# Weights times values of two attentions in plain float32, two heads side by side

## The chip, the cores and the metric

The kernel runs on one core of a Trainium2 chip. A core has a tensor engine (PE: matmuls, and PEld, its loading of the stationary operand), three engines for elementwise work (DVE, ACT and POOL) and queues of DMA. The engines run beside each other, each takes its own instructions in order, and semaphores join them. TensorE's clock has two levels, 1.2 and 2.4 GHz; the profile gives the granted share, 1.0 being 2.4. The metric is the device time of the whole program in microseconds.

## The reference, cut to what matters

Two transformer blocks over 512 tokens of 1024 features, in float32. The change lies in the two attentions of the second block, in the product of the weights with the values:

```python
# stick-breaking attention, 16 heads of 64
z = q k' / 8
log_1m = where(key < query, log_sigmoid(-z), 0)
a = where(key < query, exp(log_sigmoid(z) + sum of log_1m over later keys), 0)
o = einsum('bhqs,bshd->bqhd', a, v)                  # here

# compressed, selected and windowed attention, 16 heads in 4 groups of keys
o_cmp = einsum('bghqn,bngd->bqghd', p_cmp, v_cmp)    # here
o_sel = einsum('bghqkl,bgqkld->bqghd', p_sel, v_sel) # here
o_win = einsum('bghqs,bsgd->bqghd', p_w, v_w)        # here
out = (gate_0 o_cmp + gate_1 o_sel + gate_2 o_win) @ w_o
```

With 512 keys, the selected and the windowed attention are both causal attention over keys and values of their own (b = 0 and 1 in the kernel).

## The kernel before, in words

Features or keys lie on the 128 partitions, tokens in the free dimension. TensorE has a fast float32 (float32r, `F32R`) that takes numbers of fewer bits; the kernel makes a float32 product of it by splitting each operand into a high part (ACT copies and rounds, `xh`, `wh`) and a low part (the rest by subtraction, `xl`, `wl`) and adding three products. A matmul whose operands are plain `F32` is float32 as it stands; the profile records it as two matmuls. Weights of the projections come in 512 KB pieces (`Weights`, L303 to 369): SP issues the load of `ws`, ACT makes `wh` (L341), and DVE, for a few pieces POOL, `wl` (L350), both two pieces ahead of their use.

**Stick-breaking attention** (`s_all`). `S_ORDER` writes the order of the work out by hand: step i runs through the parts from left to right, and a part with number n handles head i - n. Each engine takes its instructions in that order. A head i of step i: the projection of queries or keys for a later pair of heads (`sproj`, 24 matmuls, evacuated by `st`, L1616, and split into `sq` or `kk`), scores on the lower triangle as 1280 columns in two parts `za` and `zb` (`s_scores`), cap at 30 (`s_cap`, DVE, L1664 and L1665), exp and ln (`s_exp`, ACT, L1670 and L1671), maximum with the scores (`s_soft`, DVE, L1677 and L1678), high parts (`s_high`, POOL, L1686 to L1688), low parts (`s_low`, L1690: 512 columns on POOL and 768 on DVE, by `low2`, L1718). One step later `s_weights` adds sums of these on PE (`sph`, `spl`), and `s_a` takes exp into `sA` (ACT, L1724 and L1725). `s_ahigh` (POOL, L1731) and `s_alow` (POOL 512 and DVE 640 columns, L1718) split the weights into `sah` and `sal`; `s_values` splits the values into `sv`, 64 columns of high parts beside 64 of low. `s_out` makes the products: for three of four blocks of keys one matmul with `sah` and one with `sal`, each 128 columns of `sv`; for the last a float32 one with `sA`. High values' products lie on partitions 0 to 63 and low values' on 64 to 127; `join` copies the one half (ACT, L1764) and adds the other (DVE, L1765). After the last heads comes the output projection, whose first products (`start`, placed by `S_LEAD` and `S_SPLIT`) stand between the steps of heads 14 and 15.

**Compressed, selected and windowed attention** (`n_attend`). A step is a chunk c of 128 queries of a head h for one of two b; chunks go in the order 3, 2, 0, 1 with 512, 384, 128 and 256 keys. `ORDER` has the parts: scores (two float32r matmuls), `n_bias` (DVE, L2094: mask, and the least), `n_exp` (ACT, L2099), `n_sums` (DVE, reciprocal), `n_scale` (POOL, L2108: gate over sum), `n_turn` (PE, L2116: transposes), `n_high` (ACT, L2126) and `n_low` (DVE, L2130), which split the transposed weights into `pts` or `pth` and `ptl`, and after the last chunk `n_out`, with two matmuls for each of four blocks of keys and two for the compressed weights (`cph`, `cpl`). `join` follows for each head, `n_head` for each pair. `g_query` prepares the queries of a pair, an instruction in each step; POOL makes their low parts (L2075). Every fourth head a step for the compressed scores (`c_`...) opens a group.

Of the kernel before, what the change touches and what calls it, by code (L numbers as in the profile page):

```python
# [18 lines left out]
P = 128  # L19
# [206 lines left out]
def _constants():  # L226
    """Tables that depend on the shapes alone: name -> [128, n]."""
# [143 lines left out]
class Norm:  # L371
    """One over the root of the mean square over the features, for tokens in the free dimension.

    The factor is applied to what the products give, so that they need not wait for it."""

    def __init__(self, s, eps, name, n=T, apart=False):
        """apart: the last squares are summed on their own."""
# [17 lines left out]
    def mean(self, src=None, more=None):  # L395
        """Mean squares with tokens on partitions, [128, chunks], before eps."""
# [32 lines left out]
    def bcast(self, tm=None, tag="rbc", bufs=2):  # L429
        """The factor along the free dimension, the same on every partition."""  # L430
# [13 lines left out]
class Norm2:  # L444
    """The norm that ends the first block and the one that opens the second, as one factor."""
# [22 lines left out]
class Kernel:  # L468
# [19 lines left out]
    def open_banks(self, stack, pool):  # L488
        """PSUM: a pool of eight banks, or banks by their places."""
# [66 lines left out]
    def group(self, ps, w, xh, xl, ks, first, last, m=P):  # L556
        """Accumulate into ps over the k tiles ks: three products of the parts."""
# [49 lines left out]
    def proj_tokens(self, name, xh, xl, chunks):  # L607
        """Products with tokens on partitions: a bank of 512 columns for each chunk."""
# [16 lines left out]
    def resid(self, k, ps, norm, gain, x):  # L625
        """Add to the residual, and what the next products need of it."""
# [13 lines left out]
    # ---- the whole  # L640
# [68 lines left out]
    # ---- block 1: state space and pooling mixer  # L709

    def _mix(self):
# [8 lines left out]
        # B0, C0 and dt come first, each as soon as what it needs is there  # L720
# [66 lines left out]
    def g_z(self, j, ps):  # L787
        """y silu(z) = y (z / 2) (1 + tanh(z / 2))"""
# [53 lines left out]
    def setup(self):  # L842
        """Tables of the state space part."""
# [17 lines left out]
    def select(self, k):  # L861
        """The rows of both heads of a pair, for 64 features each."""
# [3 lines left out]
    def stage(self, n=1):  # L866
        """A step of what runs beside the projections, at most n pairs of heads among it."""
# [14 lines left out]
    def conv(self, name=None, ps=None):  # L882
        """The next step of three convolutions under way, the middle one's first."""
# [1369 lines left out]
```

## Time and profile before

| | us |
|---|---|
| median of 3 runs (2264.5 to 2266.25) | 2265.91 |
| the profiled execution's span | 2262.3 |
| PE busy | 2161.9 |
| DVE busy | 1305.9 |
| ACT busy | 910.6 |
| POOL busy | 544.6 |

The profile is of one execution. Busy is the time in which at least one instruction of the engine ran; a matmul's record goes on after the next has begun, so spacings from start to start tell more of PE than durations. Stages are told by the time from the start of the span: stick-breaking attention with projections from 951 to about 1112 us, its end to about 1153, the compressed, selected and windowed attention from 1680 to 1848.5. A row with an arrow in brackets gives the time that the engine stood before it, and what ended that.

### The profile page before, as it was taken

What the parts mean: (1) busy time and instruction counts of PE and PEld (TensorE: products, weight loads), DVE (VectorE), ACT (ScalarE), POOL (GpSimd) and SP (SyncE); (2) the same over time, 40 slices, a digit from 0 to 9 for tenths busy, and PEclk for the clock granted to TensorE, in tenths of its full rate; (3) what the DMA queues carried; (4) which work ended last, traced back from release to release, by engine and by line L of the source; (5) the groups of instructions that cost most, each with busy time, mean ns of one, the idle gap of its engine ahead of it and who ended that gap; (6) DMA issues with size and microseconds to landing.
All of it is one profiled execution on the core that took longest, in us unless ns stands there. A gap on an engine that the chain in (4) does not pass through costs nothing.

```text
span 2262.3 us, 27154 instructions
## 1 busy us (share of the span) xinstructions
PE 2161.9 (96%) x10250; PEld 1776.0 (79%) x10250; DVE 1305.9 (58%) x2058; ACT 910.6 (40%) x1485; POOL 544.6 (24%) x559
## 2 busy tenths in 40 slices
PE   8899999999999999999899999999888899999998
PEld 5677888788888887777778888887677778888886
DVE  6988756454433335589965343445768875534333
ACT  4333534343322224366544332332448864423222
POOL 3333401111110104166630000013448851000001
PEclk9999999999999999999999999999899999999999
DMA  4222434122332223322233323323331113333231
GB/s 136 67 64 73 140 106 152 59 66 94 101 103 93 93 89 98 121 65 66 56 106 100 103 93 94 102 93 121 106 108 30 31 43 117 93 103 95 94 101 65
DMA packets 63379, 206.09 MB, mean 91 GB/s; under 512 B 7440, under 2 KB 8336, under 8 KB 63120
## 3 DMA queue, kind: packets, MB, share of 16 engines
q1 hardware_dynamic: 59504, 196.99, 27.8%
q10 hardware_dynamic: 3744, 7.37, 0.9%
q8 instruction: 80, 1.31, 0.2%
q14 instruction: 51, 0.42, 0.1%
HBM read 189.39 MB, written 6.29 MB: 86 GB/s over the span
## 4 chain that ended last, share of the span: by engine, by line
PE 68%; DVE 15%; ACT 7%; issue 5%; POOL 4%; DMA 1%; ACTq 0%; POOLq 0%; DVEq 0%
PE psum L540 53%; PE b L540 13%; DVE wl L350 2%; DVE spl L1718 1%; ACT wh L341 1%; DVE t L908 1%; POOL np L2108 1%; ACT sT L1670 1%; ACT sT L1671 1%; DVE pv L1089 1%; DVE xl L553 1%; POOL cx L1832 1%; PE psum L2116 1%; ACT xh L552 1%; DVE pts L2130 1%
## 5 line engine op out<-in xcount | busy, mean ns | idle before, releaser
L540 PE MATMUL psum<-xh,wh 128*128 128x512 f32 x1560 | 611.6, 392 | 2.3 <-ACT sA L1725 1.3
L540 PE MATMUL psum<-xh,wl 128*128 128x512 f32 x1560 | 609.4, 391 | 1.8 <-DVE wl L350 1.5
L540 PE MATMUL psum<-xl,wh 128*128 128x512 f32 x1560 | 608.8, 390 | 0.0
L341 ACT ACTIVATE wh<-ws 128x1024 fp32r<-128x1024 f32 (+1 forms) x346 | 356.3, 1038 | 384.8 <-PE psum L540 321.5
L350 DVE TENSOR_TENSOR wl<-ws,wh 128x1024 fp32r<-128x1024 f32 (+2 forms) x332 | 421.1, 1274 | 86.1 <-ACT wh L341 85.4
L540 PEld LDWEIGHTS psum<-xh,wl 128*128 128x128 f32 x1560 | 293.1, 188 | 66.3 <-DVE wl L350 4.3
L540 PEld LDWEIGHTS psum<-xh,wh 128*128 128x128 f32 x1560 | 293.3, 188 | 63.4 <-issue 1.8
L540 PEld LDWEIGHTS psum<-xl,wh 128*128 128x128 f32 x1560 | 293.3, 188 | 60.9 <-DVE xl L550 0.2
L540 PE MATMUL b<-xh,wh 128*128 128x512 f32 (+1 forms) x488 | 196.1, 402 | 8.4 <-ACT wh L341 6.6
L540 PE MATMUL b<-xh,wl 128*128 128x512 f32 (+1 forms) x488 | 193.6, 397 | 3.8 <-POOL wl L350 1.9
L540 PE MATMUL b<-xl,wh 128*128 128x512 f32 (+1 forms) x488 | 193.7, 397 | 0.5 <-DVE xl L553 0.5
L1357 DVE TENSOR_TENSOR h<-h,psum 128x512 f32<-128x512 f32 x48 | 33.1, 689 | 161.2 <-PE psum L540 161.2
L540 PE MATMUL psum<-hh,wh 128*128 128x512 f32 x320 | 125.1, 391 | 0.0
L540 PE MATMUL psum<-hh,wl 128*128 128x512 f32 x320 | 124.7, 390 | 0.0
L540 PE MATMUL psum<-hl,wh 128*128 128x512 f32 x320 | 124.6, 389 | 0.0
L1348 ACT ACTIVATE t<-t 128x512 f32<-128x512 f32 x64 | 40.5, 632 | 188.9 <-DVE t L1347 188.9
L540 PEld LDWEIGHTS b<-xh,wh 128*128 128x128 f32 (+1 forms) x488 | 92.9, 190 | 28.4 <-ACT wh L341 6.6
L540 PEld LDWEIGHTS b<-xh,wl 128*128 128x128 f32 (+1 forms) x488 | 92.8, 190 | 26.6 <-DVE wl L350 3.3
L553 DVE SCALAR_TENSOR_TENSOR xl<-h,cols,xh 128x512 fp32r<-128x512 f32 x64 | 76.6, 1212 | 61.9 <-ACT xh L552 61.9
L540 PEld LDWEIGHTS b<-xl,wh 128*128 128x128 f32 (+1 forms) x488 | 92.9, 190 | 20.5 <-DVE xl L553 1.2
L392 POOL TENSOR_TENSOR acc_final<-acc_final,sq_final 128x512 f32<-128x512 f32 x6 | 10.4, 1733 | 336.1 <-ACT sq_final L388 336.1
L1287 POOL TENSOR_TENSOR t<-t,t 128x512 f32<-128x512 f32 x22 | 28.4, 1290 | 257.2 <-DVE t L1282 232.7
(515 smaller groups left out, 3510.6 us busy)
## 6 DMA issues: line engine op xcount, KB each, us to landing
ws<-in_wst SPq DMA_DIRECT2D x332, 512.0 KB, 3.4
h<-in_xT SPq DMA_DIRECT2D x16, 256.0 KB, 3.7
kk<-kk SPq DMA_DIRECT2D x16, 256.0 KB, 3.4
nq<-nq SPq DMA_DIRECT2D x16, 256.0 KB, 2.9
ws<-in_wst SPq DMA_DIRECT2D x8, 384.0 KB, 3.1
spill<-back SPq DMA_DIRECT2D x8, 256.0 KB, 2.0
back<-spill ACTq DMA_DIRECT2D x8, 256.0 KB, 3.5
spill<-h ACTq DMA_DIRECT2D x8, 256.0 KB, 5.9
```

What stands on the lines that cost most here:

```text
L341: self.nc.scalar.activation(hi[:, :n], s, AF.Copy)
L350: e.tensor_tensor(lo[:, :n], s, hi[:, :n].bitcast(F32), op=ALU.subtract)
L540: self.nc.tensor.matmul(ps, a, b, start=start, stop=stop, skip_group_check=again)
L552: nc.scalar.activation(hi, src, AF.Copy, scale=scale)
L553: nc.vector.scalar_tensor_tensor(lo, src, scale, hi.bitcast(F32), op0=ALU.mult, op1=ALU.subtract)
L908: nc.vector.scalar_tensor_tensor(t, u[:, q:q + T], cw[:, q:q + 1], t, op0=ALU.mult, op1=ALU.add)
L1089: nc.vector.tensor_tensor(o[:, a:], src[:, a:], src[:, a - n:528 - n], op=ALU.add)
L1287: nc.gpsimd.tensor_tensor(t, t, gate[0], op=ALU.mult)
L1348: nc.scalar.activation(t, t, AF.Square)
L1357: nc.vector.tensor_tensor(self.h[:, m, :], self.h[:, m, :], ps, op=ALU.add)
L1670: self.nc.scalar.activation(t, t, AF.Exp)
L1671: self.nc.scalar.activation(t, t, AF.Ln, bias=1.0)
```

## The change

- The products of weights and values take plain float32 operands: `sA` and `vf` in the first attention, `pt`, `cp`, `vs` and `vc` in the second. The splits `s_ahigh`, `s_alow`, `s_values`, `n_low`, `c_low` and those of the values are gone, and so are `join` and `add`.
- Two heads share a bank: each matmul has 64 columns of values, and the second head's output lies on partitions 64 to 127. They are made once for two heads, after the second of them. In the first attention one ACT copy (`s_join`) then takes both heads, in the second `split` makes the high and low parts of both straight from the bank.
- `s_low` runs on POOL alone, all 1280 columns.
- In the second attention the order of the work is: two heads for b = 0, then the same two for b = 1. The transposed weights are moved by DVE for chunks 1 and 2 and by ACT for 0 and 3 (`n_move`). The low parts of the queries go from POOL (two halves) to DVE (one instruction).
- `sA` has four buffers instead of two; `pt` has three sets.

```diff
-    S_ORDER = (("proj", 0), ("scores", 0), ("low", 1), ("evac", 0), ("cap", 0), ("alow", 2),
+    S_ORDER = (("proj", 0), ("scores", 0), ("low", 1), ("evac", 0), ("cap", 0),
                ("qparts", 0), ("kparts", 0), ("exp", 0), ("soft", 0), ("high", 0),
-               ("weights", 1), ("a", 1), ("ahigh", 1), ("out", 2), ("values", 1), ("join", 2),
-               ("add", 2))
-    S_LEAD = ((14, "proj"), (14, "add"), (15, "alow"), (15, "values"), (17, "kparts"))
+               ("weights", 1), ("a", 1), ("out", 2), ("join", 2))
+    S_LEAD = ((14, "proj"), (14, "join"), (15, "cap"), (15, "out"), (17, "kparts"))
...
     def s_low(self, i):
-        self.low2(lo, t, hi, self.S_POOL[0])
+        self.nc.gpsimd.tensor_tensor(lo, t, hi.bitcast(F32), op=ALU.subtract)
...
     def s_out(self, i):
-        a, ah, al = self.hd[i]
-        vv = self.sv.pop(i)
+        if i % 2 == 0:
+            return
         ps = self.bank("bo")
-        for j in range(3):
-            v = vv[:, j, :]
+        for j in range(4):
             w = 512 - P * j
             s = slice(self.OFF[j], self.OFF[j] + w)
-            self.mm(ps[:, P * j:], v, ah[:, s], j == 0, False)
-            self.mm(ps[:, P * j:], v, al[:, s], False, False)
-        self.mm(ps[:, 384:], vv[:, 3, :].bitcast(F32), a[:, 1152:], False, True)
+            for e in range(2):
+                u = i - 1 + e
+                self.mm(ps[64 * e:64 * e + 64, P * j:], self.vf[:, j, u, :], self.hd[u][:, s],
+                        j == 0, j == 3)
...
-    ORDER = (("scores", 0), ("out", 7), ("join", 9), ("bias", 1), ("turn", 4), ("exp", 2), ("add", 9),
-             ("sums", 2), ("low", 6), ("tick", 0), ("high", 5), ("scale", 2), ("head", 13))
+    ORDER = (("scores", 0), ("out", 7), ("head", 9), ("bias", 1), ("turn", 4), ("exp", 2),
+             ("sums", 2), ("tick", 0), ("move", 5), ("scale", 2))
...
-            for s in halves:
-                nc.gpsimd.tensor_tensor(q[r, 1, s], qr[r, s], q[r, 0, s].bitcast(F32),
-                                        op=ALU.subtract)
-                yield
+            nc.vector.tensor_tensor(q[r, 1, :], qr[r, :], q[r, 0, :].bitcast(F32),
+                                    op=ALU.subtract)
...
+        if c in (1, 2):
+            self.nc.vector.tensor_copy(dst, src)
+        else:
+            self.nc.scalar.activation(dst, src, AF.Copy)
...
     def n_out(self, u):
-        if u["c"] != self.QORD[3]:
+        if u["c"] != self.QORD[3] or h % 2 == 0:
             return
...
+            for e in range(2):
+                self.mm(self.av[halves[e]], vc[:, (h - 1 + e) % 4, :], cp, True, False)
+        pt = [self.pt.pop((h - 1 + e, b)) for e in range(2)]
         for j in range(4):
-            for part in pt:
-                self.mm(self.av[:, P * j:], self.vs[:, b, j, g, :],
-                        part[:, 4 * j:3 * j + 4, :].rearrange("p c q -> p (c q)"),
-                        False, b == 1 and j == 3 and part is pt[1])
+            for e in range(2):
+                self.mm(self.av[halves[e], P * j:], self.vs[:, b, j, g, :],
+                        pt[e][:, 4 * j:3 * j + 4, :].rearrange("p c q -> p (c q)"),
+                        False, b == 1 and j == 3)
```

## Rows read from the trace of the kernel before

**Rows 1.** Stretches: us, busy (x count) of PE, PEld, DVE, ACT, POOL; clock, DMA, GB/s.
```profile
951.00:1112.00 161.00, 151.41 (x775) 121.03 (x773) 143.10 (x161) 95.58 (x124) 98.51 (x81) 0.98 0.23 66
...
1680.00:1848.50 168.50, 146.07 (x926) 119.40 (x926) 148.11 (x573) 145.72 (x427) 134.66 (x205) 0.99 0.13 30
1725.20:1767.10 41.90, 36.80 (x236) 29.95 (x237) 37.06 (x145) 36.95 (x109) 34.98 (x55) 1.00 0.13 28
```
**Rows 2.** Timeline, one step of the first attention: start us, us, instruction, [idle before].
```profile
1028.41 0.39 PE L540 MATMUL psum<-sq,kk 128*128 128x512 f32 x1
...
1030.06 0.39 PE L540 MATMUL psum<-sph,none 128*128 128x384 f32 x1
...
1030.88 0.45 PE L540 MATMUL psum<-spl,none 128*128 128x384 f32 x1 [0.44 <-DVE spl L1718]
...
1032.99 1.27 ACT L1670 ACTIVATE sT<-sT 128x1280 f32<-128x1280 f32 x1 [0.24 <-DVE sT L1665]
1033.08 0.48 PE L540 MATMUL psum<-sah,sv 128*128 128x512 f32 x1
...
1038.44 1.27 POOL L1688 TENSOR_SCALAR sph<-sT 128x1280 fp32r<-128x1280 f32 x1
1038.93 1.85 DVE L350 TENSOR_TENSOR wl<-ws,wh 128x1024 fp32r<-128x1024 f32 x1 [0.41 <-ACT wh L341]
1039.68 2.12 POOL L1731 TENSOR_SCALAR sah<-sA 128x1152 fp32r<-128x1152 f32 x1
1040.18 0.39 PE L540 MATMUL psum<-sq,kk 128*128 128x512 f32 x1
```
**Rows 3.** Timeline of PE, two places with 64-column float32 weights.
```profile
99.23 0.39 PE L540 MATMUL b<-xl,wh 128*128 128x512 f32 x1
99.46 0.39 PE L540 MATMUL b<-xh,wl 128*128 128x512 f32 x1
99.78 1.09 PE L540 MATMUL b<-d,xc 128*64 128x128 f32 x16
100.80 0.94 PE L540 MATMUL b<-ct,prev 128*128 128x128 f32 x6
...
1641.54 0.66 PE L540 MATMUL psum<-hidt,cols 128*64 128x128 f32 x8 [1.52 <-DVE hidt L1869]
```
**Rows 4.** Groups by line, whole span: count | busy us, mean ns | idle before.
```profile
L350 POOL TENSOR_TENSOR wl<-ws,wh 128x1024 fp32r<-128x1024 f32 x14 | 35.1, 2505 | 141.3 <-ACT wh L341 141.3
...
L1718 POOL TENSOR_TENSOR sal<-sA,sah 128x512 fp32r<-128x512 f32 x16 | 21.2, 1326 | 0.1
...
L350 DVE TENSOR_TENSOR wl<-ws,wh 128x1024 fp32r<-128x1024 f32 (+2 forms) x332 | 421.1, 1274 | 86.1 <-ACT wh L341 85.4
```
**Rows 5.** Timeline of PE, end of the first attention.
```profile
1100.69 0.39 PE L540 MATMUL psum<-sph,none 128*128 128x384 f32 x1
...
1108.53 0.77 PE L540 MATMUL psum<-sq,kk 128*128 128x512 f32 x1 [3.04 <-ACT h L1764]
...
1145.51 0.38 PE L540 MATMUL psum<-sA,sv 128*128 128x128 f32 x2
```
**Rows 6.** Stretches, columns as in rows 1: two behind a stop.
```profile
1107.60:1117.70 10.10, 8.81 (x30) 7.12 (x31) 9.80 (x12) 6.41 (x10) 6.95 (x6) 0.50 0.10 31
...
1643.50:1646.80 3.30, 3.30 (x12) 2.82 (x12) 2.87 (x4) 2.26 (x3) 0.00 (x0) 0.50 0.06 11
```
**Rows 7.** Groups by line, one group of four heads, 1725.2 to 1767.1.
```profile
L2130 DVE TENSOR_TENSOR ptl<-psum,pth 128x512 fp32r<-128x512 f32 (+3 forms) x16 | 7.6, 472 | 0.0
...
L1765 DVE TENSOR_TENSOR h<-h,psum 64x512 f32<-64x512 f32 x4 | 2.7, 678 | 0.1
...
L2126 ACT ACTIVATE pts<-psum 128x512 fp32r<-128x512 f32 (+3 forms) x16 | 6.8, 427 | 0.3
...
L1764 ACT ACTIVATE h<-psum 64x512 f32<-64x512 f32 x4 | 2.4, 594 | 0.1
...
L2075 POOL TENSOR_TENSOR nq<-qr,nq 64x256 fp32r<-64x256 f32 x8 | 5.8, 728 | 0.3
```

More of the change, by code (lines that the diff above doesn't have):

```diff
@@ L1480, in _stick @@
         self.s_all(norm, xh, xl)
-    S_ORDER = (("proj", 0), ("scores", 0), ("low", 1), ("evac", 0), ("cap", 0), ("alow", 2),
+    S_ORDER = (("proj", 0), ("scores", 0), ("low", 1), ("evac", 0), ("cap", 0),
                ("qparts", 0), ("kparts", 0), ("exp", 0), ("soft", 0), ("high", 0),
-               ("weights", 1), ("a", 1), ("ahigh", 1), ("out", 2), ("values", 1), ("join", 2),
-               ("add", 2))
-    S_POOL = 512, 512
-    S_BUFS = dict(sT=2, sA=2, sp=1, sa=1, st=2, back=3)
-    S_LEAD = ((14, "proj"), (14, "add"), (15, "alow"), (15, "values"), (17, "kparts"))
-    S_SPLIT = ((14, "cap"), (14, "scores"), (14, "out"), (14, "alow"), (14, "out"),
-               (14, "kparts"), (16, "ahigh"))
+               ("weights", 1), ("a", 1), ("out", 2), ("join", 2))
+    S_BUFS = dict(sT=2, sA=4, sp=1, st=2, back=3)
+    S_LEAD = ((14, "proj"), (14, "join"), (15, "cap"), (15, "out"), (17, "kparts"))
+    S_SPLIT = ((14, "cap"), (14, "scores"), (14, "out"), (14, "kparts"), (14, "out"),
+               (14, "kparts"), (16, "a"))
     def s_all(self, norm, xh, xl):
@@ L1712, in s_weights @@
         self.hd[i] = [za, zb]
-    def low2(self, lo, src, hi, n):
-        for e, c in ((self.nc.gpsimd, slice(0, n)), (self.nc.vector, slice(n, lo.shape[-1]))):
-            if c.start < c.stop:
-                e.tensor_tensor(lo[:, c], src[:, c], hi[:, c].bitcast(F32), op=ALU.subtract)
     def s_a(self, i):
@@ L1781, in _nsa @@
         ks = self.slab("ks")
-        vs = self.slab("vs").rearrange("p k t -> p (k t)").rearrange(
-            "p (b c g d) -> p b c g d", b=2, c=4, g=4)
+        half = self.slab("vs", F32).rearrange("p k t -> p (k t)")
+        vs = half[:, :2048].rearrange("p (b c g d) -> p b c g d", b=2, c=4, g=4)
+        self.pt0 = half[:, 2048:3712].rearrange("p (n q) -> p n q", q=P)
         self.ks, self.vs = ks, vs
         self.kb = ph0.tile([P, 4, 2, P], F32, name="kb")
-        self.vcs = ph0.tile([P, P], F32R, name="vcs")
+        self.vcs = ph0.tile([P, 64], F32, name="vcs")
         nc.gpsimd.memset(self.kb, 0.0)
@@ L1797, in _nsa @@
         ):
-            self.oh = self.slab("oh")
-            pts = self.slab("pts").rearrange("p k t -> p (k t)")
-            self.pts = [pts[:, 1664 * a:1664 * a + 1664].rearrange("p (n q) -> p n q", q=P)
-                        for a in range(2)]
+            self.oh, self.ol = self.slab("oh"), self.slab("ol")
             self.n_attend()
@@ L1944, in n_proj @@
         for c, ps in enumerate(pss):
-            o = self.vs[:, :, c, :, :]
-            v = ps.rearrange("p (b g d) -> p b g d", b=2, g=4)
-            for b in range(2):
-                self.split(o[:, b, :, 0:64], o[:, b, :, 64:128], v[:, b], norm.tm[:, c:c + 1])
+            nc.scalar.activation(self.vs[:, :, c, :, :],
+                                 ps.rearrange("p (b g d) -> p b g d", b=2, g=4), AF.Copy,
+                                 scale=norm.tm[:, c:c + 1])
         hid = self.gelu(pc)
@@ L2004, in n_attend @@
             steps.append(dict(g=g, c=3))
-            for h in range(4 * g, 4 * g + 4):
+            for h0 in (4 * g, 4 * g + 2):
                 for b in range(2):
-                    for c in self.QORD:
-                        steps.append(dict(g=g, h=h, b=b, c=c))
+                    for h in (h0, h0 + 1):
+                        for c in self.QORD:
+                            steps.append(dict(g=g, h=h, b=b, c=c))
         n = len(steps)
-        self.pt = {}
+        self.pt, self.npt = {}, 0
         lead = []
-        def lower(p):
-            self.nc.vector.tensor_tensor(ol[:, p, :], self.qraw[:, p, :],
-                                         self.oh[:, p, :].bitcast(F32), op=ALU.subtract)
+        ol = self.ol
         def out(k):
@@ L2117, in n_turn, with n_move @@
         u["ps"] = ps
-    def n_high(self, u):
+    def n_move(self, u):
         h, b, c = u["h"], u["b"], u["c"]
         if c == self.QORD[0]:
-            self.pt[h, b] = self.pts if b == 0 else [
-                self.tmp("pt" + a, (P, 13, P), F32R, bufs=1) for a in "hl"]
-        u["parts"] = [a[:, c:4 * c + 1:3, :] for a in self.pt[h, b]]
-        u["ps"] = u["ps"][:, :P * (c + 1)].rearrange("p (j q) -> p j q", q=P)
-        self.nc.scalar.activation(u["parts"][0], u["ps"], AF.Copy)
-    def n_low(self, u):
-        hi, lo = u.pop("parts")
-        self.nc.vector.tensor_tensor(lo, u.pop("ps"), hi.bitcast(F32), op=ALU.subtract)
+            self.pt[h, b] = self.pt0 if self.npt % 3 == 2 else self.tmp("pt", (P, 13, P), bufs=2)
+            self.npt += 1
+        dst = self.pt[h, b][:, c:4 * c + 1:3, :]
+        src = u.pop("ps")[:, :P * (c + 1)].rearrange("p (j q) -> p j q", q=P)
+        if c in (1, 2):
+            self.nc.vector.tensor_copy(dst, src)
+        else:
+            self.nc.scalar.activation(dst, src, AF.Copy)
     def n_out(self, u):
         g, h, b = u["g"], u["h"], u["b"]
-        if u["c"] != self.QORD[3]:
+        if u["c"] != self.QORD[3] or h % 2 == 0:
             return
-        pt = self.pt.pop((h, b))
+        halves = [slice(0, 64), slice(64, 128)]
         if b == 0:
@@ L2212, in c_turn, with c_move @@
         self.n_turn(u)
-    def c_high(self, u):
-        u["parts"] = [self.tmp("cp" + a, dtype=F32R, bufs=1) for a in "hl"]
-        self.nc.scalar.activation(u["parts"][0], u["ps"], AF.Copy)
-        u["cp"] = u["parts"], u.pop("vc")
-    def c_low(self, u):
-        self.n_low(u)
+    def c_move(self, u):
+        cp = self.tmp("cp", bufs=1)
+        self.nc.scalar.activation(cp, u.pop("ps"), AF.Copy)
+        u["cp"] = cp, u.pop("vc")
     def c_out(self, u):
```

52 lines of the change are left out of this document (12 added, 40 removed).

## The prediction

> **What bounds the kernel now.** I read first the table by stage, because the change touches two stages only. It cuts out the steady part of the stick-breaking attention (951 to 1112 us), the windowed and selected attention (1680 to 1848.5) and, inside that one, one full group of four heads (1725.2 to 1767.1) [rows 1]. In the first, DVE is busy 143.1 of 161 us and PE 151.4; in the second, PE 146.1, DVE 148.1, ACT 145.7 and POOL 134.7 of 168.5. So the second is not bound by one engine: all four are between 80 and 88%, and each waits for the others in turn. A busy PE counts tails of pipelined matmuls, so its real load is lower than shown.
>
> For the first stage I read one step of the order of instructions [rows 2]. From one head's scores to the next, 1028.41 to 1040.18, a step takes 11.77 us. PE spends 1.65 on the scores (to 1030.06), 3.0 on the weights (to 1033.08), of which 0.65 is a stop for `spl` (the next product could go at 1030.23 and goes at 1030.88), 1.6 on the values and 5.5 on the next projection (24 matmuls at 0.23 [rows 3]; the two together 7.1). The loop that really closes the step is longer: exponentials at 1032.99, high parts on POOL at 1038.44, and on DVE the low parts of the projection's weights (1038.93, 1.85 us) and then of softplus (`spl`, 768 columns), after which DVE takes the next projection's result and the next cap, and ACT the next exponentials. DVE is in order, so `s_low` stands in front of the next head's `s_cap`.
>
> **The change on PE.** Before, one head's values take two fp32r matmuls of 128 columns of weights for each block of keys; after, one plain float32 matmul of 64 columns, and each head has its half of the partitions. What does that cost? The trace has the very form, in the state space part: 16 records of 128*64 with 128 columns are 8 matmuls (a float32 matmul is two records), and the next thing on PE starts 1.02 us after the first [rows 3]; that is 0.128 a matmul with the switch in front and behind, and about 0.104 without (an estimate: 0.32 instead of 0.23 before the first of them, so 0.09 for the change of form on one side and as much on the other). The second such place, 8 records in 0.66 us with a tail, agrees. A head has 10 blocks of 128 columns, so its values cost 1.04 to 1.28 us; before 1.6 in the first stage and, in the second, two of 0.23, 0.18, 0.12 and 0.11, about 1.27. For two heads I take 2.1 plus 0.35 for both changes of form: 2.45 instead of 3.2 (2.9 without its stop) and 2.5. So PE gains 0.2 to 0.35 us a head in the first stage and nothing in the second.
> Here a rule speaks against the change. The Trainium skill (TensorEngine Tiling, Key Properties) says that changing the tiling mode drains TensorE. The rows show what that is worth here: about 0.1 us on a side. If a drain took a whole record of 0.39 us on each side instead, the 24 places would cost 24 x 2 x 0.3 = 14 us more.
>
> **First stage, step by step.** The step loses `sah`, `sal`, `sv` and the joins: some 3 us on POOL, and on DVE its part of `spl`, a `sal`, a `sv` and a join. DVE stops being the limit. But `s_low` now has all 1280 columns on POOL. That instruction isn't in the trace. Bounds: 1.33 us for 512 columns and 2.5 for 1024 [rows 4], so 3.1 by that slope; 3.0 if the smaller ones carry the set-up. I take 3.05.
> Let S be the end of a head's scores on PE. The cap no longer waits for `spl`, so the exponentials start about 1.5 us earlier than the S+2.93 seen (1032.99 against 1030.06); the high parts, which ended at S+9.65, end near S+8.1, and the low parts at S+11.2. There is one more: the low parts of the weights of the stream (`wl`, DVE). In the step `wl` takes 1.85 with POOL at work [rows 2] and 1.27 in the mean of all [rows 4]: when DVE reads two operands of SBUF while POOL works there, one of them stands still. In the new order `wl` comes up while POOL is at the high parts and goes in front of the low ones: 1.1 us, so L = S+12.2 in steps in which it does, S+11.2 in steps in which it comes later. The Trainium skill (SBUF — State Buffer, Who interferes with whom) has this as an exclusive lock, held for the whole instruction; the trace agrees (`sah` is issued at 1039.68 and ends at 1041.80, 1.0 us after `wl` ends at 1040.78).
> PE has now no values in even steps and two heads' in odd ones: 1.65 + 2.4 + 5.5 = 9.55 and 12.0. In an odd step the weights of the head before need its low parts, S+12.2, when PE is there at S+9.55+0.2: PE stands 2.4 us. In the even step, after 14.4 us, nothing waits. Two heads then cost 9.55 + 12.0 + 2.4 = 23.95 us, against 23.54: +0.4, seven times: +3 us. With L = S+11.2 it is 22.95: -0.6, seven times: -4. So the gain of this stage is given back by the longer low parts; I take +3, being nearest to the row with `wl`.
> The new stop has a second price. After PE stood 3.04 us before 1108.53 [rows 5], the granted clock was 0.50 (1.2 GHz) from 1107.6 to 1117.7; after the stop of 1.52 at 1641.54 [rows 3] it was 0.50 for 3.3 us from 1643.5 [rows 6]. Such a short stretch costs half its length, 1.7 us. With 2.4 us of standing in each of seven odd steps that could be 0 to 12 us; I take three of them, +5.
> The end of the stage gains. Now the last scores wait 3.04 us at 1108.53 and run at half clock after that, about 5 us more. From the end of the last scores with a projection (1100.7) to the last values (1145.51 with 0.2 to go) are 45 us [rows 5]. In the new order the weights and values before it fill that stop; adding up the same way (two heads' values 2.45, weights 2.4, the 63 matmuls of the output projection that stand between, low parts at S+11.2) I come to 40. -5 us; bounds 0 and -9.
>
> **Second stage.** One group of four heads takes 41.9 us [rows 1]. DVE loses the low parts, 7.6 twice (two rows alike), those of the compressed weights, some 0.7 (a tile as wide as a join's), and the joins' sums, 2.7 [rows 7]. It takes over half of the moves, 640 of each 1280 columns (7.5, at the rate of the same row), the queries' low parts (4 of 0.68) and the heads' low parts (2 of 0.67). 37.1 becomes 30. ACT loses half of its copies (two rows of 6.8) and the joins (2.4): 36.95 becomes 28. POOL loses the queries' low parts (5.8): 35 becomes 29. PE stays at 36.8 busy (values 10.2 before, 9.8 after).
> So three of the four engines get 17 to 24% lighter, and PE, the only one that keeps its load, becomes the limit. How much of the 41.9 goes depends on the chain through a step (scores, least, exponentials, sum, scale on POOL, turn), which isn't shorter. Bounds: nothing, if that chain sets the step, and 8.6 us a group, if PE runs without any stop: 84 turns at 0.11, the products of scores 10.3, values 12 and compressed scores 1.8 are 33.3 us (an estimate from the spacings of [rows 3]). I take half, 3.9 us, since stops for the compressed scores and for POOL's rotary work remain and since values now come in bursts of 2.5 to 3.3 us. Four groups: -15.5, bounds 0 and -34, of which I give -6 and -26 weight.
> The rest (values' parts in the projection of the stage, 16 instructions of ACT and DVE that become 4, zeroing half of `vc`) lies beside running matmuls: 0; if that cover were gone, 4 us. The slabs, the spill and the MLPs see nothing.
>
> **Sum.** 2262.3 + 3 + 5 - 5 - 15.5 = 2249.8 for a profiled execution like that of before. The median of the runs is 3.6 us above that span (2265.91), so 2253.
>
> **The rivals.** (1) PE takes both gains: `wl` stays out of the way (-4), no lower clock, second stage without stops (-24), end -5: 2229 to 2236. For it: DVE falls to 72% there. Against: the chain through POOL. (2) The chain holds the second stage as it is: -3 there, and +3, +3, -4 in the first: 2262 to 2267, no change. For it: the engines wait for each other now although none is full [rows 1]. Against: each link of the chain (sum, scale, turn) stands in a queue that becomes shorter. (3) Slower: the float32 matmuls of the two halves don't overlap when 512 columns wide, and a matmul costs twice what the rows at 128 show. A group has 96 such blocks; at 0.21 each they take 20 us instead of 10 and PE's 33 become 43, over the 41.9 of today, so it decides from about 0.2 a block on: +2 to +3 a group, +15 for eight pairs of heads in the first stage, and none of the gain: 2288 to 2300. Against: two places in the trace at the low price. The Trainium skill (FP8 and Floating Point Precision, on true FP32) counts four passes; at four full passes and no overlap it would be this case, at four with both halves at once it would be mine. (4) Slower by less: the stop in the odd steps costs a lower clock each time (+12 rather than +5) and the second stage gives only 4: 2262.3 + 3 + 12 - 5 - 4, and 3.6 more for the median: 2272.
>
> **How the numbers follow.** Forecast 0.60, rival 1 0.15, rival 2 0.12, rival 3 0.06, rival 4 0.07. The likeliest gives 2253. The range goes from the middle of rival 1 to above rival 2: 2234 to 2270; rival 3, most of rival 4 and half of rival 1 stay out, 0.2. About 0.2% (4.5 us) is what a measurement can tell: faster than 2261.4 is rival 1 and nearly all of the forecast, 0.72; slower than 2270.4 is rival 3, most of rival 4 and a little of rival 2, 0.12; between lies 0.16.
>
> **What would show it.** In the trace of the changed kernel: values at 2.1 to 2.5 us for two heads, else rival 3. In the first stage steps of about 9.5 and 14.4 us in turn, with PE standing for POOL's `spl` in the odd ones, and `spl` of 3 us, 4 with a block; no stop there, and the stage is shorter than I say. Stretches at 0.5 of the clock behind those stops. In the second stage a group of 38 us with DVE, ACT and POOL near 30 each; 33 to 34 speaks for rival 1, 41 for rival 2. The forecast is wrong if a wait appears that I don't name: for `pt` buffers (three sets for two heads), for the one bank of values, or for ACT's copies in the odd steps.

## The result and the profile after

The changed kernel takes 2276.45 us (median of 4 runs, 2274.0 to 2278.95) against 2266.08 of before: a ratio of 1.0051, 95% interval 1.0039 to 1.0064. It is 10 us slower; 13 faster were forecast, and the time lies above the range.

The profiled execution's span is 2277.1 us (before 2262.3). By stage, with PE's own instructions as marks: the changed execution is 1.7 us late at 240 us, ahead of all that the change touches; 1.8 at the end of the first attention (1145.65 before, 1147.47 after, for the same matmul); and 14.8 behind the second one (1858.70 and 1873.47). So the first attention gave and took nothing, and nearly all of the loss, 13.0 us between these two marks, belongs to the second, where 15.5 us were to be gained.

The table by stage answers [rows 1]: the first attention, the second one, one group of four heads in it, and a short stretch inside that group (us, busy and count of PE, PEld, DVE, ACT, POOL; granted clock, DMA share, GB/s).

```profile
951.00:1116.00 165.00, 149.50 (x794) 117.27 (x793) 113.39 (x114) 88.22 (x105) 75.66 (x56) 0.97 0.23 66
1688.00:1862.00 174.00, 146.89 (x903) 102.40 (x903) 124.05 (x508) 117.30 (x349) 118.67 (x177) 0.93 0.11 26
1729.90:1773.40 43.50, 37.02 (x238) 25.82 (x237) 32.08 (x130) 29.68 (x88) 30.40 (x46) 0.96 0.12 26
...
1734.00:1737.00 3.00, 2.72 (x11) 2.43 (x12) 2.37 (x11) 2.15 (x7) 2.73 (x5) 0.50 0.00 0
```

DVE, ACT and POOL did get lighter, by 5, 7 and 5 us a group. The group is longer all the same (43.5 for 41.9), and the clock, 0.99 over the second stage before, is 0.93: stretches at half clock, of which the last line is one.

The first attention, one pair of steps of the changed kernel, to be held against [rows 2]:

```profile
1045.25 0.39 PE L540 MATMUL psum<-sq,kk 128*128 128x512 f32 x1
...
1052.90 1.53 DVE L350 TENSOR_TENSOR wl<-ws,wh 128x1024 fp32r<-128x1024 f32 x1 [0.58 <-ACT wh L341]
1053.44 2.13 POOL L1686 TENSOR_SCALAR sph<-sT 128x1280 fp32r<-128x1280 f32 x1
1054.75 0.39 PE L540 MATMUL psum<-sq,kk 128*128 128x512 f32 x1
...
1055.65 2.92 POOL L1691 TENSOR_TENSOR spl<-sT,sph 128x1280 fp32r<-128x1280 f32 x1
...
1058.62 0.44 PE L540 MATMUL psum<-spl,none 128*128 128x384 f32 x1 [1.84 <-POOL spl L1691]
...
1060.98 2.37 PE L540 MATMUL psum<-sA,vf 128*64 128x512 f32 x16
...
1063.28 0.50 PE L540 MATMUL psum<-xh,wh 128*128 128x512 f32 x1
...
1064.26 2.95 POOL L1691 TENSOR_TENSOR spl<-sT,sph 128x1280 fp32r<-128x1280 f32 x1
...
1064.98 3.32 DVE L350 TENSOR_TENSOR wl<-ws,wh 128x1024 fp32r<-128x1024 f32 x1 [3.17 <-ACT wh L341]
...
1068.85 0.39 PE L540 MATMUL psum<-sq,kk 128*128 128x512 f32 x1
```

From scores to scores a step takes 9.50 (1045.25 to 1054.75) and then 14.10 us, two heads 23.60 against 23.54 of before. In each second step PE stands 1.84 us for POOL's low parts. The values of two heads take 2.30 us (1060.98 to 1063.28). Later in the same step `wl` comes up behind the next head's `spl` and takes 3.32 us: there DVE stands, and PE doesn't wait for it.

What PE waited for over the whole run (us in total, times, the longest) shows where the second attention lost. In these rows `np` is the weights of a chunk before they are transposed, `nmx` and `nsm` are its least value and its sum, and `cmx` and `csm` the maximum and the sum of the compressed scores. Before:

```profile
PE psum L2116 <- POOL np L2108: 6.2, 20, 0.4
PE psum L540 <- DVE spl L1718: 5.7, 14, 0.5
PE psum L2116 <- POOL np L2208: 5.1, 4, 2.0
```

After:

```profile
PE psum L2077 <- POOL np L2069: 19.1, 35, 2.9
PE psum L540 <- POOL spl L1691: 17.4, 9, 3.1
...
PE psum L2077 <- POOL np L2162: 7.9, 4, 2.2
```

The waits of the transposes for POOL's scaling grew from 6.2 to 19.1 us and those for the compressed weights from 5.1 to 7.9, though POOL itself had less to do. One such place, the compressed step in the timeline of the changed kernel:

```profile
1728.71 0.69 DVE L2141 TENSOR_TENSOR np<-psum,small 128x512 f32<-128x512 f32 x1 [1.14 <-PE psum L540]
...
1729.44 0.69 DVE L2143 TENSOR_REDUCE cmx<-np 128x16 f32<-128x512 f32 x1
...
1730.16 0.69 DVE L2144 TENSOR_TENSOR np<-np,cmx 128x512 f32<-128x512 f32 x1
...
1731.10 0.55 POOL L2069 TENSOR_SCALAR np<-np,nsm,gates 128x256 f32<-128x256 f32 x1 [3.22 <-DVE nsm L2064]
...
1731.61 0.69 DVE L2153 TENSOR_REDUCE csm<-np 128x16 f32<-128x512 f32 x1
1731.71 0.44 PE L2077 MATMUL psum<-small,np 128*128 128x128 f32 x2 [1.17 <-POOL np L2069]
...
1733.17 1.05 POOL L2162 TENSOR_TENSOR np<-np,csm 128x512 f32<-128x512 f32 x1 [1.52 <-DVE csm L2157]
...
1734.28 1.11 PE L2077 MATMUL psum<-small,np 128*128 128x128 f32 x4 [1.89 <-POOL np L2162]
...
1737.47 1.08 PE L540 MATMUL psum<-pt,vs 128*64 128x512 f32 x4
```

DVE makes three passes over the compressed scores in a row. The sums of the ordinary chunks stand behind them in its queue, POOL stands 3.22 us for one, and PE 1.17. Then DVE's other passes come, and PE stands 1.89 us more. The next values, work that PE could have done meanwhile, come only at 1737.47, when it is over. Before, the same passes of DVE had values of single heads beside them (timeline):

```profile
1723.36 0.69 DVE L2189 TENSOR_REDUCE cmx<-np 128x16 f32<-128x512 f32 x1
...
1723.73 0.39 PE L540 MATMUL psum<-cph,vc 128*128 128x512 f32 x1
...
1725.22 1.26 PE L540 MATMUL psum<-pts,vs 128*128 128x512 f32 x7 [0.62 <-DVE pts L2130]
...
1728.35 0.66 PE L2116 MATMUL psum<-small,np 128*128 128x128 f32 x4 [1.04 <-POOL np L2208]
```

### The profile page after: what moved, and what is told of

The parts are those of the page before. It is cut to its first block, busy times and chain, and to the rows that moved or that the text cites. A ratio compares the mean times of both kernels' runs of the same rounds, so it can differ in the third digit from the quotient of the medians.

```text
span 2277.1 us, 26704 instructions
## 1 busy us (share of the span) xinstructions
PE 2159.2 (95%) x10250; PEld 1750.3 (77%) x10250; DVE 1230.7 (54%) x1917; ACT 870.4 (38%) x1377; POOL 494.5 (22%) x495
## 3 DMA queue, kind: packets, MB, share of 16 engines
q8 instruction: 80, 1.31, 0.2%
## 4 chain that ended last, share of the span: by engine, by line
PE 74%; DVE 12%; POOL 5%; issue 4%; ACT 4%; DMA 0%; ACTq 0%; POOLq 0%; DVEq 0%; SPq 0%
PE psum L540 59%; PE b L540 12%; DVE wl L350 2%; PE psum L2077 1%; POOL spl L1691 1%; DVE t L908 1%; DVE pv L1089 1%; POOL np L2069 1%; POOL sph L1686 1%; POOL cx L1802 1%; DVE xl L553 1%; ACT xh L552 1%; ACT sT L1668 0%; ACT sT L1669 0%; DVE prev L1061 0%
## 5 line engine op out<-in xcount | busy, mean ns | idle before, releaser
L350 DVE TENSOR_TENSOR wl<-ws,wh 128x1024 fp32r<-128x1024 f32 (+2 forms) x332 | 427.0, 1291 | 105.5 <-ACT wh L341 105.2
L1348 ACT ACTIVATE t<-t 128x512 f32<-128x512 f32 x64 | 40.5, 632 | 188.9 <-DVE t L1347 188.9
L2069 POOL TENSOR_SCALAR np<-np,nsm,gates 128x512 f32<-128x512 f32 (+3 forms) x128 | 83.4, 654 | 46.8 <-DVE nsm L2064 34.1
L2077 PE MATMUL psum<-small,np 128*128 128x128 f32 x336 | 66.4, 302 | 27.2 <-POOL np L2069 19.1
```

The source lines that it names most:

```text
L350: e.tensor_tensor(lo[:, :n], s, hi[:, :n].bitcast(F32), op=ALU.subtract)
L1348: nc.scalar.activation(t, t, AF.Square)
L2069: self.nc.gpsimd.tensor_scalar(u["p"], u["p"], u.pop("sm"), self.gates[:, u["c"], e:e + 1], op0=ALU.mult, op1=ALU.mult)
L2077: self.nc.tensor.transpose(ps[:, s], p[:, s], self.ident)
```

## The experiments

**Which half.** The first attention changed and the second as before, and the other way round.

> The first attention as in the changed kernel, the second as before. Theory A (the loss lies in the second attention, where the values of two heads now come in one burst on PE): the two heads of the first attention go on taking 23.6 us as in the changed trace, its start loses 2 us at a stop for spl and its end gains 2, so the time is that of before within 3 us: 2263 to 2269. Rival B (the loss comes from both halves alike, as a price of plain float32): half of the 10 us or more are here, 2270 to 2273.

2264.63 us, ratio 1.0001 (0.9992 to 1.0010): nothing gained, nothing lost.

> The first attention as before, the second as in the changed kernel. Theory A: all of the loss is here, 2273 to 2279, the group of four heads at 43 to 45 us in place of 41.9, PE standing some 10 us in it after each burst. Rival B: 2269 to 2272.

2276.55 us, 1.0052 (1.0035 to 1.0069). The whole loss is in the second attention; B falls.

**The price of 64 columns.**

```diff
-        for j in range(4):
...
-            for e in range(2):
-                u = i - 1 + e
+        for e in range(2):
+            u = i - 1 + e
+            for j in range(4):
...
```

> The changed kernel, with all values of one head of a pair before those of the other, in both attentions, where the change has them in turn. It asks for the price of the 64 columns by itself. Theory A says that a matmul of 512 columns costs 0.42 us as the trace of the changed kernel has it, because the two heads' matmuls share PE by being in turn; one by one each would cost 0.85 at 512, a pair 4.2 us in place of 2.1, which is 8 x 2.1 = 17 us in the first attention and 16 x 2.1 and more = 34 to 40 in the second: 2315 to 2335. Rival C (a 64-column matmul costs 0.42 alone as well, the order doesn't matter): 2274 to 2279, no change.

2332.18 us (one run), 56 more than the changed kernel. The values of a pair, 2.37 us when the heads take turns, are in PE's timeline:

```profile
1016.79 4.02 PE L540 MATMUL psum<-sA,vf 128*64 128x512 f32 x16
```

The next matmul starts at 1020.74, 3.95 us after the first; 0.2 us of that lie in a stretch at half clock, and the pair at 990.22, all at full clock, takes 3.86, against 2.30 in turns. Rival C falls: with four matmuls of one half in a row the low price is gone. Strict turns aren't needed, though: in the second place of [rows 3] the code (`second`) gives two matmuls of the one half and then two of the other, and their records still start two at a time, 1641.54 and 1641.56, 1641.70 and 1641.71, at the low price.

**Are the bursts the cause?** The values of a pair in four steps instead of one:

```diff
-    ORDER = (("scores", 0), ("out", 7), ("head", 9), ("bias", 1), ("turn", 4), ("exp", 2),
...
+    ORDER = (("scores", 0), ("out", 6), ("out", 7), ("out", 8), ("out", 9), ("bias", 1),
...
+        for j in ((), (0,), (1,), (2, 3))[piece]:
```

> The changed kernel, with the values of two heads of the second attention spread over four steps (compressed part, first block, second block, the last two), and the split of the result at the end of its step, one step later. The same matmuls, no more and no fewer. Theory A: no burst over 0.9 us, so DVE, ACT and POOL don't run dry; the group falls from 43.5 to 38 to 41 us and the stretches of lower clock go, so 2255 to 2268. Rival D (the chain from scores to the transposes is too long whatever PE does meanwhile): the group stays at 43 and the time at 2272 to 2278.

2275.76 us, 1.0049 (1.0034 to 1.0064), groups of 43.9 us. My theory A, that the length of the bursts starves the other engines, fell. PE's waits for POOL's scaling did shrink, from 19.1 us to 11.6, and the clock over 1682 to 1862 us was 0.94 where the changed kernel has 0.92, but the time stayed.

**The compressed transposes, or all transposes, later.**

First the compressed ones alone, in parts of the order of their own:

```diff
-    def c_turn(self, u):
+    def c_lturn(self, u):
...
+    ORDER = (("scores", 0), ("out", 7), ("head", 9), ("bias", 1), ("turn", 4), ("lturn", 7),
+             ("exp", 2), ("sums", 2), ("tick", 0), ("move", 5), ("lmove", 8), ("lout", 8),
+             ("scale", 2))
...
```

> The changed kernel, with the transposes of the compressed weights three steps later (and their move and use), which leaves the long chain behind the compressed scores (three DVE passes, exp, four DVE passes, POOL) time to end. Theory E (what the second attention lost is one stop of PE a group for the compressed weights, 1.9 us where it was 1.0, and the stretch of half clock that follows it): the stop and the stretch go, the group falls from 43.6 to 41 or below, 2258 to 2268. Rival D (each step's own chain, from scores to transposes, holds PE): less than 3 us come back, 2273 to 2278.

2276.83 us, 1.0054 (1.0039 to 1.0069): nothing. The stop only changed its name. It was 1.89 us of a transpose waiting for POOL; now, in PE's timeline, the next scores wait for a bank that DVE's least values free:

```profile
1730.20 0.73 PE L540 MATMUL psum<-ks,nq 128*128 128x512 f32 x2 [1.61 <-DVE nmx L2056]
```

Then all of them:

```diff
-    ORDER = (("scores", 0), ("out", 7), ("head", 9), ("bias", 1), ("turn", 4), ("exp", 2),
-             ("sums", 2), ("tick", 0), ("move", 5), ("scale", 2))
...
+    ORDER = (("scores", 0), ("out", 8), ("head", 10), ("bias", 1), ("turn", 5), ("exp", 2),
+             ("sums", 2), ("tick", 0), ("move", 6), ("scale", 2))
...
```

> The changed kernel, with the transposes of every chunk, their moves, the values and the split one step later, so that the chain from scores to transposes has five steps in place of four. Theory E: helps the compressed step in part only, the stop of 1.9 us falls by about a step of 1.3, so the clock may stay up: 2262 to 2272. Rival D: all stops shrink, the group falls to 39 to 40 us, 2255 to 2263. If the lags are not what holds PE at all: 2274 to 2279.

2271.09 us, 1.0030 (1.0018 to 1.0042): 5 us back, between the two theories.

The spread values and the later compressed transposes together:

> The spread values and the later compressed transposes together. Theory E: as the later transposes alone, within 3 us. If bursts and the compressed step each cost, and hid each other: 2250 to 2258.

2275.50 us, 1.0049 (1.0034 to 1.0064): as each alone.

**The low parts of softplus**, divided as before, with only the first attention changed:

```diff
-        self.nc.gpsimd.tensor_tensor(lo, t, hi.bitcast(F32), op=ALU.subtract)
+        for e, c in ((self.nc.gpsimd, slice(0, 512)), (self.nc.vector, slice(512, 1280))):
+            e.tensor_tensor(lo[:, c], t[:, c], hi[:, c].bitcast(F32), op=ALU.subtract)
```

> Only the first attention changed, and in it the low parts of softplus divided as before (512 columns on POOL, 768 on DVE). It asks if POOL's 2.9 us for 1280 columns is what gives the first attention's gain back. Theory (as in the prediction: PE stands about 2 us in each second step for POOL): the stop goes, two heads take 21.6 to 22 us in place of 23.6, and the time falls by 11 to 14 us: 2250 to 2255. Rival (the high parts on POOL and the order on DVE hold it as they held the kernel before): 2262 to 2267.

2249.63 us, 0.9933 (0.9917 to 0.9950), inside the forecast. Two heads take 21.6 us (1037.37 to 1058.99), and the stop is gone (timeline of the first attention):

```profile
1036.80 0.96 DVE L1692 TENSOR_TENSOR spl<-sT,sph 128x768 fp32r<-128x768 f32 x1 [1.16 <-POOL sph L1686]
1036.85 2.05 POOL L1692 TENSOR_TENSOR spl<-sT,sph 128x512 fp32r<-128x512 f32 x1
1037.37 0.39 PE L540 MATMUL psum<-sq,kk 128*128 128x512 f32 x1
...
1058.99 0.39 PE L540 MATMUL psum<-sq,kk 128*128 128x512 f32 x1
```

**The compressed step under the values**, inserted four steps later in its group:

```diff
-            steps.append(dict(g=g, c=3))
...
+            part.insert(4, dict(g=g, c=3))
...
```

> The changed kernel, with the step of compressed scores four steps later in each group, so that the values of the pair before (2.3 us on PE) come right in the time in which DVE makes its seven passes for it. Theory F (the values of the last heads used to fill PE while DVE was at the compressed step; with values only after each second head they come later, and PE stands): the stops of 1.2 and 1.6 to 1.9 us a group and the lower clock behind them go, the group comes to 40 to 41.5, 2260 to 2267. Rival D (each step's own chain): group 43 to 44, 2272 to 2278.

2273.32 us, 1.0036 (1.0022 to 1.0049), groups of 42.6: 3 us back. The stops of 1.17 and 1.89 became one of 1.31, but it is still there. Theory F, that the values were the cover, holds a part of the loss only.

**Without the compressed step**, in both kernels:

> The changed kernel without the steps of the compressed attention: its scores, weights and products with the values are left out, so the output lacks that part. Theory F: without them the changed order costs nothing, and its second attention is as short as that of before without them, or shorter by some 1.5 us a group, the difference of PE's own work: a group (32 steps) of 35 to 37 us. Rival D: still longer than before by 2 us a group.

2255.76 us, a group of 38.3 (table by stretches, columns as above):

```profile
1722.10:1760.40 38.30, 34.38 (x209) 22.88 (x209) 28.25 (x122) 28.23 (x84) 29.29 (x45) 0.96 0.13 29
```

and in that group, among the waits of PE and of its loading:

```profile
PEld psum L2076 <- POOL np L2068: 7.4, 15, 1.0
...
PE psum L2076 <- POOL np L2068: 3.1, 8, 0.6
...
PE psum L540 <- DMA nq<-nq: 1.1, 2, 0.6
```

> The kernel before without the steps of the compressed attention (its scores, weights and products are left out, so the output lacks that part). PE loses 1.8 of scores, 1.8 of products and 0.5 of transposes a group, and the stops of some 1.5 us around them: a group of 36 to 38 us, the time 20 us lower, whichever theory holds; it is what the changed kernel without them is held against.

2260.36 us, a group of 39.4, the same two views:

```profile
1724.00:1763.40 39.40, 32.83 (x208) 26.39 (x209) 33.07 (x137) 36.08 (x107) 33.53 (x52) 1.00 0.13 28
```

```profile
PEld psum L2115 <- POOL np L2107: 5.4, 10, 0.7
PEld psum L540 <- DVE nsm L2102: 4.2, 3, 1.4
PE psum L540 <- DMA nq<-nq: 2.4, 2, 1.2
PEld psum L540 <- DVE ptl L2129: 2.2, 2, 1.1
PE psum L540 <- DVE ptl L2129: 1.6, 2, 0.8
...
PE psum L2115 <- POOL np L2107: 1.5, 5, 0.3
```

Leaving the step out takes 21 us from the changed kernel and 5 from the one before, where 20 were expected; these are single runs. By the group it takes 5.2 us (43.5 to 38.3) and 2.5 (41.9 to 39.4): the step costs the new order twice as much or more. A caution: with 32 steps a group the queries' copies come late (the waits for the DMA of `nq`). The changed order's group is 1.1 us the shorter, and its waits for these copies are 1.3 us the shorter (1.1 for 2.4), but its clock is 0.96 for 1.00; the group behind it, at 1.00 in both, takes 38.2 and 39.6. So even without the compressed step the relief of three engines, and all else that the new order has, is worth 1.1 to 1.4 us in these groups, in place of 3.9. The waits for `ptl` are gone (2.2 us of the loading, 1.6 of PE), that of the loading for `nsm` fell from 4.2 to 0.3, and those for POOL's scaling grew, the loading's from 5.4 to 7.4 and PE's from 1.5 to 3.1. Waits of the loading and of PE overlap and can't be added.

A try with what had helped, divided low parts, moved compressed step and longer lags:

> A try at a kernel that beats both: the changed kernel with the low parts of softplus divided between POOL and DVE again, the compressed step later in its group, and five steps from scores to transposes. From the single edits: the division took 14.5 us off the kernel with the first attention changed; the deeper order took 5 off the second attention, whose excess over before is 12. If theory F holds: 2240 to 2249; if not, 2255 to 2258.

2251.83 us, 0.9940 (0.9924 to 0.9957). It lies between the two forecasts. Of the 24.6 us under the changed kernel 14.6 are the division's; the other 10 belong to the moved step and the longer lags together, which gave 3 and 5 alone.

**DVE's passes for the compressed step, spread over the steps**: the four long ones one to a step, the three short ones together. The exp, the scaling and the transposes follow them, so these come later too; later transposes alone had changed nothing. The scores also get a buffer of their own, which wasn't tried alone; but in the second attention of the changed kernel all that DVE waited for before it wrote `np`, except 0.2 us, was PE's scores.

```diff
...
+    ORDER = (("scores", 0), ("out", 7), ("head", 9), ("bias", 1), ("max", 2), ("turn", 4),
+             ("lturn", 8), ("exp", 2), ("lexp", 4), ("sums", 2), ("sub", 3), ("lsums", 5),
+             ("rest", 6), ("tick", 0), ("move", 5), ("lmove", 9), ("lout", 9), ("scale", 2),
+             ("lscale", 6))
...
```

> The changed kernel, with the seven DVE passes of the compressed step given one or two to a step (over six steps, in a buffer of its own) in place of three and four at once; nothing else moved. Theory G (DVE's 3.3 us for the compressed step in two lumps keeps the next chunks' least values back, and PE stands for what follows): the stops of 1.2 and 1.9 us at the head of each group shrink below 0.7, the lower clock behind them goes, a group takes 40 to 41.5 us and the time is 2260 to 2267. Rival (the compressed step costs by PE's own 3.5 us for it): 2273 to 2278.

2266.09 us, 1.0005 (0.9996 to 1.0015): all of the loss is back. The second attention and one group in it, the group at full clock (table by stretches):

```profile
1688.00:1852.00 164.00, 139.79 (x902) 95.23 (x901) 124.08 (x508) 116.57 (x349) 120.77 (x178) 0.99 0.12 27
1724.60:1765.90 41.30, 35.94 (x238) 24.48 (x237) 31.93 (x129) 29.43 (x90) 30.81 (x47) 1.00 0.12 28
```

The timeline of DVE has its passes apart, 1.6 us from one to the next:

```profile
1726.63 0.69 DVE L2142 TENSOR_TENSOR npc<-psum,small 128x512 f32<-128x512 f32 x1 [0.97 <-PE psum L540]
1728.25 0.68 DVE L2147 TENSOR_REDUCE cmx<-npc 128x16 f32<-128x512 f32 x1
1729.86 0.67 DVE L2151 TENSOR_TENSOR npc<-npc,cmx 128x512 f32<-128x512 f32 x1
1731.69 0.67 DVE L2160 TENSOR_REDUCE csm<-npc 128x16 f32<-128x512 f32 x1
```

And of PE's waits over the whole run the one for the compressed weights fell from 7.9 us to 0.6, while the one for the scaling of ordinary chunks is as it was in the changed kernel:

```profile
PE psum L2079 <- POOL np L2071: 19.7, 41, 3.0
...
PE psum L2079 <- POOL npc L2172: 0.6, 1, 0.6
```

**Is it a loop over the steps that holds the rest?**

The longer lags, first without the compressed step, then in the kernel with only the first attention changed, then with the spread passes:

> The changed kernel without the compressed steps (that part of the output is left out), with five steps instead of four between scores and transposes. Theory H (a loop over five steps, from one transpose on PE over scores, DVE, ACT, DVE and POOL to the transposes four steps later, sets 1.19 us a step; with one step more in it the same time is shared by six): a group of 32 steps falls from 38.2 to 33 to 36 us and the time to 2240 to 2248. If something else holds the step (a unit's own queue): 37.5 to 38.5 us, 2253 to 2257.

2256.40 us, groups of 38.1 to 38.7: theory H fell.

> The best so far (only the first attention changed, low parts of softplus divided: 2249.6) with the second attention as before, but all from the transposes on one step later. Theory H would give 1 to 2.5 us a group: 2240 to 2246. If the old order isn't held by that loop: 2248 to 2252.

2256.74 us, 0.9968 (0.9957 to 0.9979): 7 us worse than with the old lags. One step more doesn't help where no lump has to be bridged, and in the old order it costs.

> The changed kernel with the divided low parts, the compressed step's DVE passes one by one, and one step more before the transposes. With theories G and H: 2238 to 2246, which would beat all others; with G wrong: 2251 to 2257.

2250.00 us, 0.9934 (0.9917 to 0.9950): short of the forecast for G and H together, as H is wrong.

**POOL's rotary work**, a third of it moved to DVE:

```diff
-            nc.gpsimd.tensor_tensor(qr[:, s], qr[:, s], sh[:, s], op=ALU.add)
+            nc.vector.tensor_tensor(qr[:, s], qr[:, s], sh[:, s], op=ALU.add)
```

> The kernel with the compressed step's DVE passes spread (2266.1), and in it the last of three rotary passes of the queries on DVE in place of POOL (4 of 0.73 us a group on POOL become 4 of some 0.4 on DVE). Theory I (the stops that are left are POOL's queue in the steps with rotary work, about 3 us a group): 1 to 2 us a group go, 2258 to 2263. Rival (not POOL's queue; DVE, with four more instructions, is what the others wait for): 2265 to 2270.

2263.90 us, 0.9996 (0.9986 to 1.0005): 2 us under the kernel that it was made from, with intervals that overlap, so the time doesn't bear out theory I. The trace shows a part of it: from one `cmx` to the next there are 40.5 and 40.2 us (1725.55, 1766.00, 1806.21), with the passes spread alone 41.3 and 41.4. That is about 1 us a group (one execution each), the lower end of what theory I gave.

The same with the divided low parts:

> The same with the low parts of softplus divided between POOL and DVE. The division gave 14.5 us, so 14 to 15 less than the run before: 2243 to 2249 with theory I, 2250 to 2255 with its rival; the best so far are 2249.6 and 2250.0.

2248.01 us, 0.9928 (0.9913 to 0.9943). It beats both kernels, by 17 and 28 us. Nearly all of it is the division of the low parts; from the first attention alone (2249.63) it can't be told apart.

## Why the prediction was wrong

**Right: the price of the values.** 2.45 us for two heads, measured 2.30 in the first attention. Rival 3 didn't come; the run one by one shows that it would have, at 4.02 us, had the halves not taken turns. That the first place of [rows 3] gave the right price was in part luck: in the code before its matmuls take turns too (`pd`, first the one half, then the other), as in the new order, but the prediction didn't ask for that condition. The Trainium skill (TensorEngine Tiling (Array Packing), Key Properties) says that tiles can run matmuls in parallel; 2.30 us in turns, for 4.02 one head after the other, agrees.

**Right in form: the first attention.** Steps of 9.5 and 14.4 us were forecast, 9.50 and 14.10 came; PE stands for POOL's `spl`, 1.84 us (2.4 forecast), as `spl` takes 2.92 (3.05) and `wl` holds back the high parts (2.13 for 1.27). The Trainium skill (SBUF — State Buffer, Who interferes with whom) has the order of issue decide which engine stands; here `wl` was issued 0.54 us ahead of `sph`, and POOL stood; for the next head `spl` was issued 0.72 us ahead of `wl`, and DVE stood (3.32 us), so the trace agrees both ways. Seven pairs of heads cost 0.4 us, for +3. The dividing run shows what that step costs: without the long `spl`, the kernel is 14.6 us faster than before.

**Wrong, with small sizes: clock and end of the first attention.** +5 for stops that lower the clock: over the steady steps (1000 to 1100) the granted clock is 1.00. -5 for the end: with the second attention as before, the kernel is 1.0 us late at the last full step and level at 1145.65, so -1. The first steps, which the sum left out, cost about 0.8 (from 956.66 to 981.48 before, from 956.43 to 982.06 with the first attention changed). Forecast in all +3, measured 0.3 (2264.63 against 2264.3), which is no difference: the total came nearer than its terms.

**Wrong: the second attention, -15.5.** The step that failed is "I take half, 3.9 us a group". It had two faults.
The first is its basis. Of the 8.6 us between 41.9 and PE's own 33.3 I gave 3.9 to three lighter engines, with no wait named that would go. They give little: without the compressed step the group is 1.1 to 1.4 us shorter than that of before, much of which goes with a shorter wait for the copies, and with the step's passes spread it is 0.6 us shorter. Rival 2's price for this stage (nearly nothing) was right on this; its cause, a chain that holds the stage, is not shown. What does hold it is open: not the length of the bursts, not the lag from scores to transposes; POOL's rotary work holds about 1 us a group of it.
The second is a term that wasn't in the sum at all. The compressed step's DVE passes, 3.3 us in two lumps, stop every chunk behind them, and the new order pays for that: spread over the steps they cost 10.4 us less. Why the old order paid less is argued and only in part shown. There a head's values, due every fourth step, lay beside the passes; now values come every eighth step and left PE open. But the values put back beside the passes gave 3 of the 10 us, and no run spreads the passes in the old order. I had the rows (the stop of 1.04 us for the compressed weights is in the trace of before) and named "stops for the compressed scores" as something that remains, but didn't ask what lay beside them and whether the new order moves that away. How much of the 10.4 us is standing and how much the half clock behind it, no run separates; both vanish together. PE's waits for the compressed weights fell by 7.3 us. The clock, 0.93 of 174 us and then 0.99 of 164, is 10.5 us of lost time if PE had worked all through these stretches, an estimate that bounds it from above; and the run with the spread values had less half clock and was no faster.

**The rivals.** The time is slower by 0.5%, which had 0.12. None of the three waits that I named as signs of being wrong is the one that came. Rival 4 had lower clocks as the cause, but in the first attention. The bound "nothing, if that chain sets the step" was no bound: a reordering can lose where it gains nothing, and the lower end for the second stage had to reach above zero by the stops that it lays bare.

## What to carry to other kernels

When a change moves a block of work in an engine's order, list what that block stood beside, above all the places where another engine has several instructions in a row: the block may have been their cover. Whether it was is a run of its own. Four engines at 80 to 88% that wait for each other didn't become faster here when three of them got lighter; before a gain is put into a sum, name the one wait that would go, and make a run that takes it away. Where a stop only changes its name when its consumer is moved, look at the producer's queue; here spreading the producer's instructions over the steps was the cure; and where one part of a change takes the gain of another, as the undivided low parts did here, the parts are worth trying apart.

## What the runs showed of the hardware

- Plain float32 matmuls with 64 columns of weights cost 0.6 of the price when those for the two halves of the output partitions stand in turns: a pair of heads' values takes 2.30 us from its start to the next matmul's, and 3.86 with four blocks of one head before those of the other, both at full clock. Two matmuls of one half before two of the other still overlapped (1641.54, [rows 3]).
- Where DVE subtracts two tiles of SBUF beside POOL, the one that starts later stands: `wl` first, POOL's high parts take 2.13 us for 1.27 in [rows 2]; POOL's `spl` first, `wl` takes 3.32, for 1.27 in the mean of [rows 4]. POOL's 512 columns of low parts beside DVE's 768 take 2.05; the same width of `sal` took 1.33 [rows 4].
- A stop of 1.84 us on PE every 23.6 us left the clock at 1.00 in the first attention, while in the second it fell to 0.50 behind the stops of 1.17 and 1.89 us that ended at 1731.71 and 1734.28. That isn't a rule: with the compressed transposes later, stops of 1.18 and 1.61 us left it at 1.00 in one group (1727.9 to 1737.0) and went with 0.50 in the next (1773.5 to 1780.0).
